# A decoder layer on one core: gates by tanh, differential-head products in token layout, work moved from VectorE to ScalarE

## The chip, the cores and the metric

The kernel runs on one core of one Trainium2 chip. The metric is the device time of one execution in microseconds (us). Before the change it is 731.5 us, the median of three runs (731.49 to 732.18).

A core has five instruction streams that run side by side and wait for one another through semaphores: TensorE (PE; its weight loads are shown apart as PEld), VectorE (DVE), ScalarE (ACT), GpSimd (POOL) and SyncE (SP, which here only issues weight transfers). Each stream is executed in its own order.

## The reference, cut to what matters

One layer, 512 tokens by 1024 features in float32. Two attention branches work on the same normalised input, are gated, merged, and followed by a gated MLP with a short convolution:

```python
h = rms_norm(x, g_mix)
z = h @ w_in                     # q, k, v of both branches and the gate logits gl
ya = swa_sink_attention(...)     # 8 heads, window 128, each query block sees 1 or 2 key blocks
ob = diff_attention(...)         # 4 heads, full causal: (softmax1 - lam * softmax2) @ v, v is 128 wide
yb = rms_norm(ob, subln_b) * (1 - lam_init)      # over the 128 features of a head, per token
gates = sigmoid(gl)
mixed = gates[0] * (ya @ w_br_a) + gates[1] * (yb @ w_br_b)
x = x + mixed @ w_o
h = rms_norm(x, g_ffn)
x = x + (silu(conv_g) * conv_v) @ w_down         # conv3 over h @ w_up
```

## The kernel before, in words

Every large product is done to float32 accuracy with three float32r matmuls: an operand is split into a high part (ACT, `whi`, line 123) and a low part (DVE or POOL, `wlo`, line 124), and `mm3` (lines 145 to 147) adds high*high, low*high and high*low. Weights come in units of 128x1024 through three raw buffers; a unit is split one unit ahead of its use.

Only TensorE's order is written out by hand. The other engines' instructions are ordered by the framework's scheduler, except where `issue_after` holds one behind another.

While attention runs, TensorE is kept supplied by a *filler*, the `Stream` object `fs`: a list of generators (gate projections, differential q/k/v projections, branch-A output, early branch-B output) that gives three 512-column matmuls per step. The table `FILL` says how many steps stand at each place between attention instructions. Its total is fixed by the work; the table only deals it out.

The stages, with the lines that the change touches:

- Sliding-window attention (8 units of a query block and a key/value head): `swa_score` (exponentials on ACT, line 581; the multiply by the reciprocal row sum, line 588, on DVE), `swa_trans` (transposes, line 597), `swa_av`.
- Gates: `gate(c)` projects one 128-feature chunk, and DVE multiplies it by the token norm into a buffer `g`. `sigmoids` (line 486) later applies the sigmoid in place: eight chunks as one block between the two attention stages, eight at the end of the second. `issue_after` keeps them behind the exponentials.
- Differential attention (16 units of head h and query block b): `diff_score` (line 683 exponentials, line 688 multiply by -lam over the sum, line 689 the difference), `diff_trans` (transposes, line 705, then the split into `ath`, line 712, and `atl`, line 713), and, once per head, `diff_av` (line 725: twelve matmuls of 512, 384, 256 and 256 columns, the values as weights, result with features on the partitions). A token's norm then needs a sum over partitions: `diff_rms` sums by matmuls with ones (line 173), and `diff_out` spreads the reciprocal root over the free axis with diagonal matrices (line 193) and two matmuls (line 194), then multiplies (line 740).
- `k_parts` builds key operands with a half copied across partitions by DVE (line 438).
- `mix` multiplies the second gate by the branch-B product (line 849), adds, splits; `resid` adds the input (line 876).

Of the kernel before, what the change touches and what calls it, by code (L numbers as in the profile page):

```python
# [62 lines left out]
FILL = dict(v=[9, 17, 25, 33], m=[0, 0, 0, 0], r=[4, 9, 13, 18], o=[7, 11, 15, 17], e=[1, 1, 0, 40], kv=4, up=3,  # L63
            warm=8, q=7, k=19, k2=4, s1=[0, 3, 2, 2, 2, 3, 3, 0, 0, 3], s2=[4, 3, 0, 3, 1, 7, 5, 2, 0, 1],
            s3=[3, 0, 1, 5, 6, 2, 2, 6, 0, 1], p0=4, p1=5, p2=8, ud=6, pd=[8, 9], f=[9, 0],
            a=[5, 1, 8, 7, 10, 2, 0, 3, 0, 1, 7, 4, 6, 0, 0, 5],
            b=[6, 2, 4, 4, 2, 7, 2, 1, 2, 0, 2, 0, 1, 1, 2, 2], c=[7, 0, 0, 1], d=[1, 0, 0, 5])
# [5 lines left out]
def tile_decoder_layer(ctx: ExitStack, tc: tile.TileContext, x4, wall, cst_d, relb_d, oneh_d, xn_d, out):  # L73
# [411 lines left out]
    def sigmoids(c0):  # L485
        return [nc.scalar.activation(G[c], G[c], AF.Sigmoid) for c in range(c0, c0 + 8)]
# [71 lines left out]
    swa_acts = []  # L558

    def swa_score(b, n):  # L560
# [22 lines left out]
        swa_acts.append(nc.scalar.activation(sk, sk, AF.Exp))  # L583
# [3 lines left out]
        for j in range(4):  # L587
            nc.vector.tensor_scalar(s[:, j, :W], s[:, j, :W], rc[:, j:j + 1], None, ALU.mult)
# [17 lines left out]
    def swa_av(b, n):  # L606

        if n == 0:
            swa_o[b] = otile()
        u = swa_o[b]  # L610
        ps = at()
        pT = swa_p.pop((b, n))
        for i, (t, h, _) in enumerate(pT):
            nc.tensor.matmul(ps, vhl[:, t, n, :], h, start=i == 0, stop=False)  # L614
        for i, (t, _, l) in enumerate(pT):
            nc.tensor.matmul(ps, vah[:, t, n, :], l, start=False, stop=i == len(pT) - 1)
        s, o = halves[n]
# [41 lines left out]
    exps = []  # L659

    def diff_score(h, b):
# [20 lines left out]
        for c in range(2):  # L682
            exps.append(nc.scalar.activation(p[:, c, :N], p[:, c, :N], AF.Exp, bias=nmx[:, c:c + 1],
                                             accum_out=sm[:, c:c + 1]))
# [3 lines left out]
        nc.vector.tensor_scalar(p[:, 1, :N], p[:, 1, :N], rc[:, 1:2], None, ALU.mult)  # L688
# [3 lines left out]
    def diff_trans(h, b):  # L692
        p = dp.pop((h, b))
        if b == 0:


            ath = at3.tile([P, 1664], F32R, tag="ath", name=nm("ath"), bufs=1)
            atl = at3.tile([P, 1664], F32R, tag="atl", name=nm("atl"), bufs=1)
            nc.gpsimd.memset(ath[:, 1408:1536].bitcast(F32), 0.0)
            nc.gpsimd.memset(atl[:, 1408:1536].bitcast(F32), 0.0)  # L700
            dt[h] = ath, atl
        ath, atl = dt[h]
# [3 lines left out]
        psv = ps[:, :(b + 1) * P].rearrange("p (a b) -> p a b", b=P)  # L706

        def cols(f):
            a = f[:, b * P:b * P + 1]
            return bass.AP(a.tensor, a.offset, [a.ap[0], (384, b + 1), (1, P)])  # L710

        nc.scalar.activation(cols(ath), psv, AF.Copy)
        nc.vector.tensor_tensor(cols(atl), psv, cols(ath.bitcast(F32)), ALU.subtract)
# [3 lines left out]
    def diff_av(h):  # L717
        ath, atl = dt.pop(h)
        po = at()

        for i, (part, at_) in enumerate(((0, ath), (1, ath), (0, atl))):
            for kb in range(NT):
                q0 = min(kb * P, 256)
                c0 = kb * 384 + q0
                nc.tensor.matmul(po[:, q0:S], vb[kb][part][:, h * P:(h + 1) * P], at_[:, c0:c0 + S - q0],  # L725
                                 start=i == 0 and kb == 0, stop=i == 2 and kb == NT - 1)
        sq = otile()
        nc.scalar.activation(sq, po, AF.Square)
        o = otile()
        nc.scalar.activation(o, po, AF.Copy, scale=gsub)  # L730
        dpo[h] = o, sq

    def diff_rms(h):
        o, sq = dpo[h]
        dpo[h] = o, token_rsqrt(token_sums(sq, lambda: fs.fill(1)), P)

    def diff_out(h):
        o, col = dpo.pop(h)
        r = along_free(col, otile, lambda: fs.fill(FILL["m"][h]))
        nc.vector.tensor_tensor(o, o, r, ALU.mult)  # L740
        nc.scalar.activation(ybt[0][:, h, :], o, AF.Copy)
        nc.vector.tensor_tensor(ybt[1][:, h, :], o, ybt[0][:, h, :].bitcast(F32), ALU.subtract)
# [26 lines left out]
    sig = ExitStack()  # L769
    with tc.issue_after(swa_acts[-1].ins), tc.issue_after(swa_acts[-2].ins):  # L770
        for i in sigmoids(0):
            sig.enter_context(tc.issue_after(i.ins))
# [5 lines left out]

    def products(place):
        for h in range(4):  # L780
            if FILL["v"][h] == place:
                fs.until("vb")
                diff_av(h)
                fill("c", h)

    todo = [(h, b) for h in range(4) for b in range(NT)]
    for i in range(len(todo) + 1):
# [25 lines left out]
    sig.close()  # L813
    fs.until("gb")
    with tc.issue_after(exps[-1].ins), tc.issue_after(exps[-2].ins), tc.issue_after(exps[-3].ins):
        sigmoids(8)
# [31 lines left out]
    def mix(c, ps):  # L848
        nc.vector.tensor_tensor(G[8 + c], ps, G[8 + c], ALU.mult)  # L849
# [22 lines left out]
    def resid(c, ps):  # L872
# [3 lines left out]
        nc.vector.tensor_tensor(t, ps, xr, ALU.add)  # L876
# [183 lines left out]
```

## Time and profile before

| | |
|---|---|
| median of three runs | 731.5 us |
| profiled execution, its own time | 730.34 us |
| its span, first to last instruction | 728.6 us |
| mean granted TensorE clock | 0.993 of full |
| PE busy | 705.9 us (97%) |
| DVE, ACT, POOL busy | 450.0, 316.0, 167.0 us |

Matmuls are pipelined: one 512-column matmul is shown with 0.39 us, but the next starts 0.23 us after it. What a matmul costs a full queue is therefore the distance between starts, and a duration is that plus the time its result takes to come out. A time in square brackets is how long the engine sat idle before the instruction, and which engine's instruction ended that.

### The profile page before, as it was taken

What the parts mean: (1) busy time and instruction counts of PE and PEld (TensorE: products, weight loads), DVE (VectorE), ACT (ScalarE), POOL (GpSimd) and SP (SyncE); (2) the same over time, 40 slices, a digit from 0 to 9 for tenths busy, and PEclk for the clock granted to TensorE, in tenths of its full rate; (3) what the DMA queues carried; (4) which work ended last, traced back from release to release, by engine and by line L of the source; (5) the groups of instructions that cost most, each with busy time, mean ns of one, the idle gap of its engine ahead of it and who ended that gap; (6) DMA issues with size and microseconds to landing.
All of it is one profiled execution on the core that took longest, in us unless ns stands there. A gap on an engine that the chain in (4) does not pass through costs nothing.

```text
span 728.6 us, 8960 instructions
## 1 busy us (share of the span) xinstructions
PE 705.9 (97%) x3312; PEld 582.6 (80%) x3312; DVE 450.0 (62%) x940; ACT 316.0 (43%) x522; POOL 167.0 (23%) x130
## 2 busy tenths in 40 slices
PE   8999999789999999989999999999999999999998
PEld 5888788668887778768888888888888888888888
DVE  5787797737429898685448877676676674322220
ACT  6554666854236446334426444444444442121220
POOL 1145253254446220274300210110110110000000
PEclk9999999989999999999999999999999999999999
DMA  8762202032221110235421332323323223333310
GB/s 315 289 207 88 87 30 88 0 116 87 72 99 62 58 59 30 87 107 167 132 87 58 116 117 91 111 86 96 107 87 102 101 80 101 125 107 108 109 66 30
DMA packets 21820, 74.04 MB, mean 102 GB/s; under 512 B 2612, under 2 KB 3152, under 8 KB 21648
## 3 DMA queue, kind: packets, MB, share of 16 engines
q1 hardware_dynamic: 18976, 65.02, 26.4%
q0 software_dynamic: 1360, 6.34, 2.6%
q10 hardware_dynamic: 1440, 2.11, 0.8%
q8 instruction: 26, 0.43, 0.2%
q14 instruction: 18, 0.15, 0.1%
HBM read 71.34 MB, written 4.47 MB: 104 GB/s over the span
## 4 chain that ended last, share of the span: by engine, by line
PE 78%; DVE 8%; issue 2%; ACT 2%; POOL 0%; DVEq 0%; ACTq 0%; POOLq 0%
PE pj L145 24%; PE pj L147 24%; PE pj L146 24%; PE at L725 1%; DVE g L850 1%; PE at L597 1%; PE at L444 1%; DVE g L849 1%; DVE o L193 1%; PE at L443 1%; DVE p L678 1%; DVE p L689 1%; PE at L705 1%; PE at L614 0%; DVE wlo L124 0%
## 5 line engine op out<-in xcount | busy, mean ns | idle before, releaser
L123 ACT ACTIVATE whi<-raw 128x1024 fp32r<-128x1024 f32 (+1 forms) x117 | 121.8, 1044 | 174.8 <-PE pj L146 115.9
L145 PE MATMUL pj<-xg,whi 128*128 128x512 f32 x480 | 189.6, 395 | 0.0
L147 PE MATMUL pj<-xg,wlo 128*128 128x512 f32 x480 | 187.3, 390 | 0.0
L146 PE MATMUL pj<-xg,whi 128*128 128x512 f32 x480 | 187.2, 390 | 0.0
L124 DVE TENSOR_TENSOR wlo<-raw,whi 128x1024 fp32r<-128x1024 f32 (+1 forms) x84 | 103.4, 1234 | 81.9 <-ACT whi L123 81.8
L147 PEld LDWEIGHTS pj<-xg,wlo 128*128 128x128 f32 x480 | 90.2, 188 | 19.2
L146 PEld LDWEIGHTS pj<-xg,whi 128*128 128x128 f32 x480 | 90.4, 188 | 17.7
L145 PEld LDWEIGHTS pj<-xg,whi 128*128 128x128 f32 x480 | 90.3, 188 | 17.5
L124 POOL TENSOR_TENSOR wlo<-raw,whi 128x1024 fp32r<-128x1024 f32 x33 | 79.6, 2418 | 96.2 <-ACT whi L123 86.7
L145 PE MATMUL pj<-whi,xg 128*128 128x512 f32 (+1 forms) x156 | 59.5, 382 | 6.0 <-ACT whi L123 5.9
L916 DVE TENSOR_TENSOR u<-pj,rbc 128x512 f32<-128x512 f32 x44 | 30.2, 689 | 48.3 <-PE pj L147 48.3
L146 PE MATMUL pj<-wlo,xg 128*128 128x512 f32 (+1 forms) x156 | 58.2, 373 | 1.7 <-POOL wlo L124 1.7
L147 PE MATMUL pj<-whi,xg 128*128 128x512 f32 (+1 forms) x156 | 58.1, 372 | 0.1
L145 PEld LDWEIGHTS pj<-whi,xg 128*128 128x128 f32 x156 | 29.8, 191 | 11.3 <-ACT whi L123 6.0
L919 ACT ACTIVATE yc<-u,cst 128x512 f32<-128x512 f32 x44 | 35.5, 810 | 4.5 <-DVE u L916 4.5
L145 PE MATMUL pj<-y,whi 128*128 128x512 f32 (+1 forms) x95 | 37.0, 390 | 0.0
L147 PE MATMUL pj<-y,wlo 128*128 128x512 f32 (+1 forms) x95 | 36.3, 382 | 0.2 <-POOL wlo L124 0.2
L147 PE MATMUL pj<-qv,wlo 128*128 128x512 f32 (+1 forms) x94 | 35.4, 377 | 1.1 <-DVE wlo L124 1.1
L146 PE MATMUL pj<-y,whi 128*128 128x512 f32 (+1 forms) x95 | 36.2, 381 | 0.0
L921 DVE SCALAR_TENSOR_TENSOR yc<-u,cst,yc 128x510 f32<-128x510 f32 x44 | 34.8, 794 | 1.3
L146 PEld LDWEIGHTS pj<-wlo,xg 128*128 128x128 f32 x156 | 29.9, 191 | 7.0 <-POOL wlo L124 2.2
L145 PE MATMUL pj<-qv,whi 128*128 128x512 f32 (+1 forms) x94 | 35.4, 376 | 0.0
(213 smaller groups left out, 1151.3 us busy)
## 6 DMA issues: line engine op xcount, KB each, us to landing
raw<-in_w_dram SPq DMA_DIRECT2D x109, 512.0 KB, 3.3
raw<-in_w_dram SPq DMA_DIRECT2D x8, 384.0 KB, 3.1
scr<-scr POOLq DMA_DIRECT2D x1, 2304.0 KB, 11.4
xnat<-in_xn_dram SPq DMA_DIRECT2D x2, 1024.0 KB, 9.4
tmp<-in_x_dram POOLq DMA_DIRECT2D x8, 256.0 KB, 3.2
g<-in_x_dram SPq DMA_DIRECT2D x7, 256.0 KB, 6.7
out_dram<-x ACTq DMA_DIRECT2D x7, 256.0 KB, 2.0
bias_a<-scr POOLq DMA_DIRECT2D x1, 1024.0 KB, 7.3
```

What stands on the lines that cost most here:

```text
L123: nc.scalar.activation(hi[:, :width], raw[:, :width], AF.Copy)
L124: eng.tensor_tensor(lo[:, :width], raw[:, :width], hi[:, :width].bitcast(F32), ALU.subtract)
L145: nc.tensor.matmul(ps, a[0], b[0], start=start, stop=False)
L146: nc.tensor.matmul(ps, a[0], b[1], start=False, stop=False)
L147: nc.tensor.matmul(ps, a[1], b[0], start=False, stop=stop)
L193: nc.vector.tensor_scalar(dg[:, t * P:(t + 1) * P], ident, part[:, t:t + 1], None, ALU.mult)
L443: nc.tensor.matmul(ps, q[:, qsl], kh[:, ksl], start=True, stop=False)
L444: nc.tensor.matmul(ps, q[:, qsl], kl[:, ksl], start=False, stop=True)
L597: nc.tensor.transpose(ps[:, j * P:(j + 1) * P], s[:, j, kb * P:(kb + 1) * P], ident)
L916: nc.vector.tensor_tensor(u, ps, rbc2, ALU.mult)
L919: nc.scalar.activation(y, u, AF.Identity, bias=cst[:, C_CB + ch:C_CB + ch + 1], scale=cw[2])
L921: nc.vector.scalar_tensor_tensor(y[:, 2:S], u[:, 0:S - 2], cw[0], y[:, 2:S], ALU.mult, ALU.add)
```

## The change

- The sigmoid is computed as (1 + tanh(x/2))/2. The tanh is issued with each gate chunk; the "+1" is joined to the multiply that uses the gate (`scalar_tensor_tensor`), and the half is applied once in `resid`. The two blocks of sigmoids and the `issue_after` around them go.
- A differential head's product is done per unit (h, b): the transposed probabilities are the weights, the values move, 128 columns each, and the result has tokens on the partitions. The sum of squares comes from ACT's accumulator; the reciprocal root scales per partition (two blocks on ACT, two on DVE); four transposes bring a head back to features on partitions, and the split out of PSUM applies the per-feature gain.
- Half of the sliding-window multiplies, the multiply by -lam over the sum, and the copies across partitions in `k_parts` move from DVE to ACT.
- `ath` and `atl` are three buffers of 512 columns instead of one of 1664 each; eight short POOL memsets go.
- `FILL` is dealt out anew. The number of filler matmuls is the same.

```diff
+        for k, (s, o) in zip(kh, halves):
+            nc.scalar.activation(k[o, :], ps[s, :], AF.Copy, scale=g[s])
         for k, l, (s, o) in zip(kh, kl, halves):
-            nc.vector.tensor_copy(k[o, :], k[s, :].bitcast(F32))
...
         nc.vector.tensor_tensor(t, ps, rbc, ALU.mult)
+        nc.scalar.activation(t, t, AF.Tanh, scale=0.5)
...
-            nc.vector.tensor_tensor(G[c], ps, G[c], ALU.mult)
+            nc.vector.scalar_tensor_tensor(G[c], G[c], 1.0, ps, ALU.add, ALU.mult)
...
         for j in range(4):
-            nc.vector.tensor_scalar(s[:, j, :W], s[:, j, :W], rc[:, j:j + 1], None, ALU.mult)
+            if j % 2:
+                nc.scalar.activation(s[:, j, :W], s[:, j, :W], AF.Copy, scale=rc[:, j:j + 1])
+            else:
+                nc.vector.tensor_scalar(s[:, j, :W], s[:, j, :W], rc[:, j:j + 1], None, ALU.mult)
...
-        nc.vector.tensor_scalar(p[:, 1, :N], p[:, 1, :N], rc[:, 1:2], None, ALU.mult)
+        nc.scalar.activation(p[:, 1, :N], p[:, 1, :N], AF.Copy, scale=rc[:, 1:2])
...
+    def diff_av(h, b):
+        ath, atl = dt.pop((h, b))
+        if b == 0:
+            dpo[h] = otile(), stat.tile([P, NT], F32, tag="oss", name=nm("oss"))
+        o, ss = dpo[h]
+        po = at()[:, :P]
         for i, (part, at_) in enumerate(((0, ath), (1, ath), (0, atl))):
-            for kb in range(NT):
-                q0 = min(kb * P, 256)
-                c0 = kb * 384 + q0
-                nc.tensor.matmul(po[:, q0:S], vb[kb][part][:, h * P:(h + 1) * P], at_[:, c0:c0 + S - q0],
+            for kb in range(b + 1):
+                nc.tensor.matmul(po, at_[:, kb * P:(kb + 1) * P], vb[kb][part][:, h * P:(h + 1) * P],
...
+        ob = o[:, b * P:(b + 1) * P]
+        nc.scalar.activation(ob, po, AF.Square, accum_out=ss[:, b:b + 1])
+        nc.scalar.activation(ob, po, AF.Copy)
 
     def diff_rms(h):
-        o, sq = dpo[h]
-        dpo[h] = o, token_rsqrt(token_sums(sq, lambda: fs.fill(1)), P)
+        o, ss = dpo[h]
+        r = token_rsqrt(ss, P)
+        for b in range(NT):
+            ob = o[:, b * P:(b + 1) * P]
+            if b % 2:
+                nc.vector.tensor_scalar(ob, ob, r[:, b:b + 1], None, ALU.mult)
+            else:
+                nc.scalar.activation(ob, ob, AF.Copy, scale=r[:, b:b + 1])
 
     def diff_out(h):
-        r = along_free(col, otile, lambda: fs.fill(FILL["m"][h]))
-        nc.vector.tensor_tensor(o, o, r, ALU.mult)
+        for b in range(NT):
+            nc.tensor.transpose(ps[:, b * P:(b + 1) * P], o[:, b * P:(b + 1) * P], ident)
+        nc.scalar.activation(ybt[0][:, h, :], ps, AF.Copy, scale=gsub)
...
-        nc.vector.tensor_tensor(t, ps, xr, ALU.add)
+        nc.vector.scalar_tensor_tensor(t, ps, 0.5, xr, ALU.mult, ALU.add)
```

Of the table, the entry for the steps after each product (`c`) went from four numbers to sixteen, and a new entry says from which unit on products start:

```diff
-            b=[6, 2, 4, 4, 2, 7, 2, 1, 2, 0, 2, 0, 1, 1, 2, 2], c=[7, 0, 0, 1], d=[1, 0, 0, 5])
+            b=[6, 2, 4, 4, 2, 7, 2, 1, 2, 2, 0, 0, 1, 4, 2, 2], c=[3, 0, 0, 0, 2, 0, 0, 0, 2, 1, 0, 0, 1, 0, 0, 0],
+            d=[1, 0, 0, 5], v0=4)
```

How instructions moved, at three places. Line numbers of the changed kernel differ by a few; in a row stand the line, the operation, the destination, its sources and the shape of the destination, on matmuls the shape streamed.

First, ScalarE between the two attention stages, before the change: the last key parts of the second differential head, the sigmoids of the first eight gates (`g`), the high part of a weight unit (`whi_1611`), the exponentials of the first differential unit (`p`).

```order
L436 ACTIVATE qv_1588<-at_1580,cst 64x512
L486 ACT_TABLE_LOAD
L486 ACTIVATE g_666<-g_666 128x512
...
L486 ACTIVATE g_1526<-g_1526 128x512
L123 ACTIVATE whi_1611<-raw_1609 128x1024
L683 ACT_TABLE_LOAD
L683 ACTIVATE p_1639,dsm_1641<-p_1639,dnmx_1650 128x128 x2
```

After the change, the same place:

```order
L476 ACTIVATE g_1507<-g_1507 128x512
...
L437 ACTIVATE qv_1595<-at_1588,cst 64x512
L437 ACTIVATE qv_1596<-at_1588,cst 64x512
L439 ACTIVATE qv_1595<-at_1588,cst 64x512
L439 ACTIVATE qv_1596<-at_1588,cst 64x512
L124 ACTIVATE whi_1711<-raw_1709 128x1024
L685 ACTIVATE p_1651,dsm_1653<-p_1651,dnmx_1662 128x128 x2
L690 ACTIVATE p_1651<-p_1651,drc_1666 128x128
```

The two table loads and the eight sigmoids are gone from between the key parts and the weight unit; two copies of key parts (L439) and the multiply by -lam over the sum (L690) are new. The eighth tanh (L476) stands earlier, among the last sliding-window instructions.

Second, TensorE at the last differential head's product, before the change (once per head; `at_3008` is the result, `ath` and `atl` the moving parts, `vbh` and `vbl` the weights):

```order
L725 MATMUL at_3008<-ath_2831,vbh_1830 128x512
L725 MATMUL at_3008<-ath_2831,vbh_1834 128x384
L725 MATMUL at_3008<-ath_2831,vbh_1838 128x256
L725 MATMUL at_3008<-ath_2831,vbh_1842 128x256
L725 MATMUL at_3008<-ath_2831,vbl_1831 128x512
...
L725 MATMUL at_3008<-atl_2832,vbh_1842 128x256
```

After the change, one unit's product is an own group (this is head 2, block 3; a head has groups of 3, 6, 9 and 12), close behind the transposes (L701) of the same unit and the scores (L445, L446) of the next:

```order
L701 MATMUL at_2891<-ident,p_2766 128x128 x4
L445 MATMUL at_2901<-qv_2582,qv_2569 128x256
L446 MATMUL at_2901<-qv_2580,qv_2569 128x256
L445 MATMUL at_2905<-qv_2583,qv_2570 128x256
L446 MATMUL at_2905<-qv_2581,qv_2570 128x256
L718 MATMUL at_2918<-vbh_1830,ath_2889 128x128
L718 MATMUL at_2918<-vbh_1834,ath_2889 128x128
...
L718 MATMUL at_2918<-vbh_1842,atl_2890 128x128
```

The values have become the moving operand, every matmul has 128 columns, and no filler stands between these transposes and the product that needs them.

Third, ScalarE at that same unit, before the change: the split `ath` of the transposes follows a weight unit, and the evacuation of the product (L728, L730) stands behind it.

```order
L683 ACTIVATE p_2740,dsm_2742<-p_2740,dnmx_2751 128x128 x2
L123 ACTIVATE whi_2907<-raw_2905 128x1024
L712 ACTIVATE ath_2555<-at_2787 128x4x128
L728 ACTIVATE o_2807<-at_2794 128x512
L730 ACTIVATE o_2809<-at_2794,gsub 128x512
```

After the change, the evacuation of the previous unit's product (L721 the squares, L722 the copy) stands ahead of the split (L702):

```order
L721 ACTIVATE o_2729,oss_2730<-at_2877 128x128
L722 ACTIVATE o_2729<-at_2877 128x128
L702 ACTIVATE ath_2889<-at_2891 128x512
L685 ACTIVATE p_2898,dsm_2900<-p_2898,dnmx_2909 128x256 x2
L690 ACTIVATE p_2898<-p_2898,drc_2913 128x256
L721 ACTIVATE o_2729,oss_2730<-at_2918 128x128
L702 ACTIVATE ath_2933<-at_2935 128x128
```

ScalarE now does two evacuations per unit instead of two per head, and the split that TensorE waits for is queued behind them.

## Rows read from the trace of the kernel before

**Rows 1.** The page: each engine's busy time, its share of the span, and its instructions.

```profile
PE 705.9 (97%) x3312; PEld 582.6 (80%) x3312; DVE 450.0 (62%) x940; ACT 316.0 (43%) x522; POOL 167.0 (23%) x130
```

**Rows 2.** The view of waits, TensorE only: whom it waited for, us in total, times, longest.

```profile
PE pj L145 <- ACT whi L123: 5.9, 1, 5.9
PE pj L146 <- POOL wlo L124: 1.7, 1, 1.7
PE at L597 <- DVE s L588: 1.5, 1, 1.5
PE pj L146 <- POOL qv L853: 1.4, 2, 0.7
PE at L705 <- DVE p L689: 1.3, 2, 1.0
...
PE at L444 <- DVE qv L439: 1.0, 2, 0.5
PE at L194 <- DVE o L193: 0.7, 1, 0.7
PE at L725 <- ACT ath L712: 0.7, 1, 0.7
PE at L443 <- DVE qv L438: 0.6, 2, 0.4
```

**Rows 3.** The timeline from 140 to 153 us, PE, ACT and POOL: start, duration, engine, line.

```profile
140.18 1.28 ACT L486 ACT_TABLE_LOAD   x1
...
140.57 0.27 PE L444 MATMUL at<-qv,qv 128*128 128x128 f32 x1
...
141.48 4.26 ACT L486 ACTIVATE g<-g 128x512 f32<-128x512 f32 x8
...
145.65 1.04 ACT L123 ACTIVATE whi<-raw 128x1024 fp32r<-128x1024 f32 x1
...
146.74 0.79 PE L145 MATMUL pj<-whi,xg 128*128 128x512 f32 x1 [5.89 <-ACT whi L123]
...
149.22 0.79 PE L146 MATMUL pj<-wlo,xg 128*128 128x512 f32 x1 [1.69 <-POOL wlo L124]
...
152.25 0.40 PE L147 MATMUL pj<-whi,xg 128*128 128x512 f32 x1
```

**Rows 4.** Timelines of TensorE alone, for the distances between starts: 128-column float32r matmuls (from 70.39; five starts from 70.39 to 70.95) and the filler behind them, eight transposes (103.83 to 104.62), one head's product (186.29 to 188.25), plain filler (188.25 to 188.48), and a token sum between filler matmuls (192.81 to 193.50: two filler matmuls and one sum).

```profile
70.39 0.28 PE L444 MATMUL at<-qv,qv 128*128 128x128 f32 x1
...
70.95 0.27 PE L443 MATMUL at<-qv,qv 128*128 128x128 f32 x1
...
71.17 0.45 PE L145 MATMUL pj<-whi,xg 128*128 128x512 f32 x1
71.46 0.40 PE L146 MATMUL pj<-wlo,xg 128*128 128x512 f32 x1
...
103.83 1.03 PE L597 MATMUL at<-ident,s 128*128 128x128 f32 x8
104.62 0.48 PE L145 MATMUL pj<-xg,whi 128*128 128x512 f32 x1
...
186.29 0.80 PE L725 MATMUL at<-ath,vbh 128*128 128x512 f32 x4
...
188.25 0.40 PE L145 MATMUL pj<-y,whi 128*128 128x512 f32 x1
188.48 0.39 PE L146 MATMUL pj<-y,whi 128*128 128x512 f32 x1
...
192.81 0.40 PE L147 MATMUL pj<-y,wlo 128*128 128x512 f32 x1
...
193.50 0.39 PE L146 MATMUL pj<-y,whi 128*128 128x512 f32 x1
```

**Rows 5.** Groups of instructions with shapes kept apart: count, busy us, mean ns of one, idle time before.

```profile
L588 DVE TENSOR_SCALAR s<-s,rc 128x256 f32<-128x256 f32 x24 | 6.8, 350 | 0.1
...
L588 DVE TENSOR_SCALAR s<-s,rc 128x128 f32<-128x128 f32 x8 | 6.1, 828 | 0.1
...
L683 ACT ACTIVATION_READ_ACCUMULATOR p<-p,dnmx 128x1 f32 x32 | 6.0, 187 | 0.0
...
L881 DVE SCALAR_TENSOR_TENSOR xg<-x,cst,xg 128x512 fp32r<-128x512 f32 x8 | 6.0, 746 | 0.0
...
L849 DVE TENSOR_TENSOR g<-pj,g 128x512 f32<-128x512 f32 x8 | 5.1, 679 | 2.4 <-PE pj L863 2.4
...
L683 ACT ACTIVATE p<-p,dnmx 128x128 f32<-128x128 f32 x8 | 3.1, 394 | 2.7 <-DVE dnmx L681 2.6
...
L712 ACT ACTIVATE ath<-at 128x512 fp32r<-128x512 f32 x4 | 2.4, 598 | 8.0 <-PE at L705 7.9
...
L712 ACT ACTIVATE ath<-at 128x256 fp32r<-128x256 f32 x4 | 1.6, 400 | 1.9 <-PE at L705 1.8
...
L712 ACT ACTIVATE ath<-at 128x128 fp32r<-128x128 f32 x4 | 1.1, 270 | 4.6 <-issue 4.6
```

**Rows 6.** One stretch of 15 us: busy time of PE, PEld, DVE, ACT and POOL (with instruction counts), granted clock, DMA share, GB/s.

```profile
240.00:255.00 15.00, 14.37 (x73) 12.55 (x74) 11.57 (x41) 8.11 (x18) 3.75 (x5) 0.89 0.16 63
```

**Rows 7.** The timeline of DVE at the last head's norm: its first instruction (the mean square), and the one behind its last.

```profile
296.15 0.16 DVE L180 TENSOR_SCALAR tv<-at 128x4 f32<-128x4 f32 x1 [3.00 <-PE at L173]
...
298.52 0.17 DVE L187 CAST colh<-y 128x4 fp32r<-128x4 f32 x1
```

More of the change, by code (lines that the diff above doesn't have):

```diff
@@ L482, in br_a @@
                 yield
-            nc.vector.tensor_tensor(G[c], ps, G[c], ALU.mult)
-    def sigmoids(c0):
-        return [nc.scalar.activation(G[c], G[c], AF.Sigmoid) for c in range(c0, c0 + 8)]
+            nc.vector.scalar_tensor_tensor(G[c], G[c], 1.0, ps, ALU.add, ALU.mult)
     class Stream:
@@ L693, in diff_trans @@
         p = dp.pop((h, b))
[L694 to L702, printed above, removed]
+        N = (b + 1) * P
+        ath = at3.tile([P, S], F32R, tag="ath", name=nm("ath"), bufs=3)
+        atl = at3.tile([P, S], F32R, tag="atl", name=nm("atl"), bufs=3)
         ps = at()
@@ L733, in diff_rms @@
-    def diff_rms(h):
-        o, sq = dpo[h]
-        dpo[h] = o, token_rsqrt(token_sums(sq, lambda: fs.fill(1)), P)
-    def diff_out(h):
-        o, col = dpo.pop(h)
-        r = along_free(col, otile, lambda: fs.fill(FILL["m"][h]))
-        nc.vector.tensor_tensor(o, o, r, ALU.mult)
-        nc.scalar.activation(ybt[0][:, h, :], o, AF.Copy)
-        nc.vector.tensor_tensor(ybt[1][:, h, :], o, ybt[0][:, h, :].bitcast(F32), ALU.subtract)
+        nc.scalar.activation(ath[:, :N], ps[:, :N], AF.Copy)
@@ new lines, in diff_trans @@
+        nc.vector.tensor_tensor(atl[:, :N], ps[:, :N], ath[:, :N].bitcast(F32), ALU.subtract)
+        dt[h, b] = ath, atl
+    dpo = {}
+    def diff_av(h, b):
[4 more added lines that the diff above has]
+        po = at()[:, :P]
+        for i, (part, at_) in enumerate(((0, ath), (1, ath), (0, atl))):
+            for kb in range(b + 1):
+                nc.tensor.matmul(po, at_[:, kb * P:(kb + 1) * P], vb[kb][part][:, h * P:(h + 1) * P],
+                                 start=i == 0 and kb == 0, stop=i == 2 and kb == b)
+        ob = o[:, b * P:(b + 1) * P]
+        nc.scalar.activation(ob, po, AF.Square, accum_out=ss[:, b:b + 1])
+        nc.scalar.activation(ob, po, AF.Copy)
@@ new lines, in diff_rms @@
+    def diff_rms(h):
+        o, ss = dpo[h]
[6 more added lines that the diff above has]
+                nc.scalar.activation(ob, ob, AF.Copy, scale=r[:, b:b + 1])
+    def diff_out(h):
+        o, _ = dpo.pop(h)
+        ps = at()
+        for b in range(NT):
+            nc.tensor.transpose(ps[:, b * P:(b + 1) * P], o[:, b * P:(b + 1) * P], ident)
+        nc.scalar.activation(ybt[0][:, h, :], ps, AF.Copy, scale=gsub)
+        nc.vector.scalar_tensor_tensor(ybt[1][:, h, :], ps, gsub, ybt[0][:, h, :].bitcast(F32), ALU.mult,
+                                       ALU.subtract)
@@ L768, in tile_decoder_layer @@
     fs.until("ga")
[L769 to L772, printed above, removed]
     fs.parts += [("vb", project(U_VB, 512, vbb), lambda: vb_parts(vbb))]
@@ L777, in tile_decoder_layer @@
     fill("p2")
[L779 to L784, printed above, removed]
     todo = [(h, b) for h in range(4) for b in range(NT)]
@@ L798, in tile_decoder_layer @@
         if i > 0:
-            products(2 * i)
+            for u, hb in enumerate(todo):
+                if u < len(todo) - 1 and max(u + 2, FILL["v0"]) == i:
+                    fs.until("vb")
+                    diff_av(*hb)
+                    fill("c", u)
             diff_trans(*todo[i - 1])
             fill("b", i - 1)
-            products(2 * i + 1)
+            if i == len(todo):
+                diff_av(*todo[-1])
         for step, at_unit in ((diff_rms, FILL["r"]), (diff_out, FILL["o"])):
@@ L812, in tile_decoder_layer @@
                         fs.parts += [("bb", br_b_early(), None)]
-    sig.close()
     fs.until("gb")
-    with tc.issue_after(exps[-1].ins), tc.issue_after(exps[-2].ins), tc.issue_after(exps[-3].ins):
-        sigmoids(8)
     fs.until("bb")
@@ L848, in mix @@
     def mix(c, ps):
-        nc.vector.tensor_tensor(G[8 + c], ps, G[8 + c], ALU.mult)
+        nc.vector.scalar_tensor_tensor(G[8 + c], G[8 + c], 1.0, ps, ALU.add, ALU.mult)
         nc.vector.tensor_tensor(G[c], G[c], G[8 + c], ALU.add)
```

33 lines of the change are left out of this document (8 added, 25 removed).

## Prediction

> **What bounds the kernel now.** I read the page first: TensorE is busy 97% of the span, every other engine under 63% [rows 1]. So time is gained only where TensorE has nothing to do, works at the lower clock, or has less to do. The view of waits for TensorE alone comes second: it puts names on the idle time. The largest by far is one wait of 5.9 us for the high part of a weight unit on ScalarE, with 1.7 us behind it for the low part on GpSimd; the rest are many waits of 0.2 to 1.5 us for DVE in the two attention stages, and some in the merge [rows 2]. The timeline around the large one comes third. The reader is to see there that TensorE's last matmul starts at 140.57, that ScalarE loads a table and computes eight sigmoids meanwhile, and that the weight unit's high part starts only at 145.65 [rows 3]. Last come the distances between starts, the price of a matmul on a full queue: 0.23 us for 512 columns, 0.112 for 128 columns ((70.95 - 70.39)/5), 0.10 for a 128-column transpose (0.79/8) [rows 4].
>
> **The change part by part.** The sum is made against the profiled execution, 730.3 us, which is 1.2 below the median of 731.5; the 1.2 is added again at the end.
>
> *The block of sigmoids: -9.7.* From 140.57 to 152.25 TensorE issues the matmul at 140.57 and eight filler matmuls, worth 0.11 + 8 x 0.23 = 2.0 us; 11.7 have passed [rows 3]. So 9.7 are lost: the wait for the high part, the wait for the low part that POOL can only begin after it, and a restart below full clock. In the changed order there is neither table load nor sigmoid between the key parts and the weight unit. The eight tanh stand one by one behind their gate chunks, each like a sigmoid (4.26 us for eight, start to end [rows 3]), in a stage where TensorE has filler. What is late next: the key parts of two differential heads, now eight copies on ScalarE instead of four there and four on DVE, and behind them on ScalarE's queue the weight unit `whi_1711` and the first exponentials. The table deals ten filler steps (ten times 0.69 us) and sixteen transposes (1.6 us) over them, so I price this at zero, and at +5 if that cover fails. A tanh can also hold ScalarE's queue while it waits for DVE's multiply; then the next weight unit is late. It is ordered one unit ahead, so zero, up to 1 us each time otherwise. SyncE's weight loads keep their order; a load that waited for a buffer held through the stall starts earlier. POOL loses eight short memsets that nobody waited for: zero.
>
> *Sliding-window attention: -1.5.* TensorE waits 1.5 us for the multiply of line 588 [rows 2], which takes four DVE instructions per unit. Two go to ScalarE and run beside the other two. A 256-column multiply took 0.350 us on DVE, a 128-column one 0.828; a ScalarE copy of those widths out of PSUM took 0.400 and 0.270 [rows 5]. I take the whole wait as gone; the bounds are 0 and -1.5.
>
> [...]
>
> *Differential attention, waits: -2.9.* The old waits there are 1.3 for the difference `p`, 1.0 and 0.6 for key parts, 0.7 for line 193 and 0.7 for `ath`: 4.3 [rows 2]. [...] In that stage DVE sheds the multiply of line 688, the key copies, the eight diagonal multiplies per head and line 740; so I let all 5.9 go.
>
> New waits come in their place. A unit's product needs `ath` from ScalarE, and the unit before it puts a square with accumulator and a copy out of PSUM ahead of it. Where no filler stands between (head 2, block 3), TensorE has four transposes and four 256-column scores to do, 0.40 + 0.48 = 0.9 us by the starts; ScalarE has 0.394 + 0.187 + 0.270, then the split, 0.598 [rows 5]: 1.45, and some 0.16 until a result is out (0.39 shown against 0.23 between starts [rows 4]). So TensorE waits 0.7. The next unit, with one filler step there, I put at 0.7 too. Queued behind a waiting product are the next unit's transposes and scores, and on ScalarE its exponentials. Other units have two to nine steps of filler there: zero. A head's four transposes wait for the norm, twelve small DVE instructions that took 298.52 - 296.15 = 2.4 us [rows 7], and for two scalings on ScalarE at 0.27 each [rows 5]. At the last head that makes, with square and accumulator, 3.5 us and three hand-overs of 0.16, so 4.0, against fifteen filler matmuls, 3.45: 0.5, and all of the merge stands behind it. At head 2 the scalings queue behind two 384-column exponentials: 1.1. Sum of the new ones 3.0; bounds 0 and 22 (see the rivals).
>
> *TensorE's own work: +2.9.* Products: 120 matmuls of 128 columns x 0.112 = 13.4, against 4 x (188.25 - 186.29) = 7.8: +5.6. Token sums: two filler matmuls with one sum between took 0.69, so a sum is worth 0.23; 16 go: -3.7. The eight matmuls of line 194 at 0.23: -1.8. Sixteen transposes at 0.10: +1.6. Behind a 128-column group the first filler matmul takes 0.29 instead of 0.23; twenty such groups: +1.2 [rows 4]. For the products the bounds are half a 128-column distance, 0.06 (if loading the weights hid fully), which is -6.2, and the 0.112 that every such row shows; a load that did not overlap at all would be +9, but no row has that.
>
> [...]
>
> *Merge: +0.5.* Eight multiplies become `scalar_tensor_tensor`: 0.746 against 0.679 us [rows 5], in a stretch where TensorE waits for the chain of DVE and POOL (1.4 us for the split of line 853 alone [rows 2]): 8 x 0.067. In the residual eight more lie beside 24 matmuls each: zero. The wait itself stays.
>
> Sum: -9.7 - 1.5 - 2.9 + 2.9 + 0.5 = -10.7. 730.3 - 10.7 = 719.6, plus 1.2: 720.8 us.
>
> **The rivals.**
>
> *Slower: ScalarE's queue sets the pace.* Each of 16 units now crosses from DVE to ScalarE and back once more, for the multiply by -lam over the sum, and has two evacuations on ScalarE. If every unit made TensorE wait 0.7 us for `ath` and 0.7 for `p`, the new waits would be 22.4 instead of 3.0: 720.8 + 19.4 = 740.2. It turns the result slower from 0.86 us per unit on (3.0 + 10.7 = 13.7, over 16). For it: ScalarE's queue is in order, and a weight unit of 1.04 us [rows 3] can stand ahead of any of these steps. Against it: ScalarE was busy 8.1 of 15 us at 240 to 255 [rows 6], and most units have filler to cover. [...]
>
> *Half: the stall only moves.* The block of sigmoids goes, but what stood behind it, key parts and the low part on POOL (2 to 3 us after the high part: 149.22 against 146.74 [rows 3]), is late itself by half of 9.7, and DVE's old waits are replaced in full by ScalarE's: 720.8 + 4.85 + 2.9 = 728.6. For it: the weight unit's place in the order is still behind all key parts.
>
> *More: no new waits, and products closer.* New table and buffers hide all of it: 720.8 - 3.0 = 717.8, and at 0.09 us per product matmul, between the bounds, 715.
>
> *No change: the block was covered.* If whatever follows had been late anyway, the 9.7 buy nothing and the rest cancels: 731. Against it: TensorE's other waits in that view are 7.2 us together, spread over both attention stages and the merge [rows 2], so little else was due just then.
>
> **How the numbers follow.** Forecast 0.60, half 0.15, more 0.12, slower 0.09, no change 0.04. The likeliest one gives 720.8; its own range is 717 to 725. The range for 8 in 10 takes in "more" at its lower end and "half" at its upper: 714 to 729. About 0.2% (1.5 us) is what a measurement of this kernel can tell from no change: faster by over that 0.86, within it 0.05, slower 0.09.
>
> **What would show it.** In the changed kernel's waits, line 123's successor should be gone as a wait of several us, and no stretch between 135 and 165 us should show TensorE under 14 us busy of 15. Line 718's 128-column matmuls should start 0.11 us apart. TensorE should wait for lines 702 and 730 to 732, together some 3 us, and no longer for the key parts. DVE's busy total should fall and ScalarE's rise. Wrong would be the forecast if TensorE waited for lines 690, 691 or 702 in most units, or if the stage from the first differential scores to the merge took longer than before.

## The result, and the profile after

The changed kernel takes 721.9 us (median of 4 runs, 721.64 to 723.62), the kernel before beside it 731.8 (4 runs): a ratio of 0.9867, 95% interval 0.9848 to 0.9886. The forecast was 720.8. The profiled execution took 721.64 us with a span of 719.7, against 730.34 and 728.6 before: 8.7 us less, where the prediction's sum, made on that execution, had 10.7.

The page, as in [rows 1]: VectorE lost 24.5 us of busy time, ScalarE gained 23.8, and TensorE's share rose to 98%.

```profile
PE 704.2 (98%) x3360; PEld 583.8 (81%) x3360; DVE 425.5 (59%) x862; ACT 339.8 (47%) x609; POOL 164.8 (23%) x122
```

The view of waits, TensorE only, which answers to [rows 2]:

```profile
PE at L718 <- ACT ath L702: 2.2, 1, 2.2
PE at L701 <- DVE p L691: 1.6, 2, 1.3
PE pj L147 <- POOL qv L843: 1.4, 2, 0.7
...
PE at L617 <- ACT pth L603: 0.8, 2, 0.5
PE at L446 <- DVE qv L441: 0.8, 1, 0.8
...
PE at L600 <- DVE s L591: 0.4, 1, 0.4
```

The 5.9 us for the weight unit and the 1.7 for its low part are gone. The wait for the multiply of the sliding-window stage fell from 1.5 to 0.4 us. The merge's 1.4 us stands unchanged. New at the top is one wait of 2.2 us for `ath`, in one unit of sixteen. The wait for line 193 is gone. The view has none for lines 730 to 732 either, which the prediction had named.

Windows of 15 us, with the columns of [rows 6]. The stretch of the old stall (135 to 165) runs at full clock. So does 240 to 255, which was at 0.89. The lower clock now stands from 270 to 285, behind the wait for `ath`. From 135 to 150 TensorE is busy 13.68 us, a little under the 14 that the prediction had named as a sign.

```profile
135.00:150.00 15.00, 13.68 (x71) 11.31 (x69) 9.52 (x18) 11.68 (x20) 5.53 (x6) 1.00 0.16 56
150.00:165.00 15.00, 15.00 (x69) 12.45 (x70) 11.13 (x34) 8.81 (x19) 6.64 (x3) 1.00 0.23 79
...
240.00:255.00 15.00, 15.00 (x82) 12.87 (x81) 10.74 (x43) 12.21 (x30) 3.43 (x3) 1.00 0.16 55
...
270.00:285.00 15.00, 14.98 (x73) 12.27 (x72) 10.53 (x47) 10.15 (x32) 0.00 (x0) 0.89 0.14 44
```

To put all of it on one scale, I took from each distance between two starts on TensorE what the shape takes on a full queue (0.227 us for 512 columns, 0.119 for 256, 0.111 for 128, 0.1085 for a 128-column transpose, 0.64 for four matmuls of an old product). What is left over is time lost to waits, to the clock and to changes of shape. What was taken off adds up to TensorE's own work. This is worked out from the timelines and good to about 1 us (the same work comes out at 690.0 to 691.5), and kernels of other length shift a little against the bounds of a stretch.

| kernel | lost 60–135 us | 135–160 | 160–335 | own work | median ratio to before |
|---|---|---|---|---|---|
| before | 3.6 | 9.8 | 15.1 | 690.6 | 1 |
| changed | 4.4 | 1.8 | 10.7 | 693.1 | 0.9867 |
| tanh alone | 3.7 | 6.0 | 16.6 | 690.1 | 0.9954 |
| filler numbers alone | 3.2 | 11.9 | 15.2 | 690.8 | 1.0009 |
| tanh and these numbers | 4.1 | 1.5 | 14.7 | 691.5 | 0.9909 |
| changed, sigmoids back | 3.2 | 14.1 | 12.3 | 693.7 | 1.0055 |
| changed, multiplies back on VectorE | 4.3 | 1.0 | 10.3 | 693.1 | 0.9856 |
| changed, old table | 4.4 | 5.9 | 14.9 | 693.2 | 0.9989 |
| changed, old layout | 4.1 | 1.8 | 28.9 | 690.8 | 1.0083 |
| the same, old places | 4.4 | 1.8 | 25.9 | 690.0 | 1.0030 |
| the same, and multiplies back | 4.1 | 1.0 | 26.9 | 690.4 | 1.0049 |

From before to changed: own work +2.5, the stretch of the stall -8.0, what lies behind it -4.4, the sliding-window stage +0.8; with the rest, +0.2, this is the span's -8.9.

### The profile page after: what moved, and what is told of

Same layout as the page of the kernel before. It is cut to its first block, busy times and chain, and to the rows that moved or that the text cites. A ratio compares the mean times of both kernels' runs of the same rounds, so it can differ in the third digit from the quotient of the medians.

```text
span 719.7 us, 9050 instructions
## 1 busy us (share of the span) xinstructions
PE 704.2 (98%) x3360; PEld 583.8 (81%) x3360; DVE 425.5 (59%) x862; ACT 339.8 (47%) x609; POOL 164.8 (23%) x122
## 4 chain that ended last, share of the span: by engine, by line
PE 87%; ACT 5%; DVE 5%; issue 1%; DMA 1%; SPq 0%; ACTq 0%; DVEq 0%
PE pj L146 27%; PE pj L148 27%; PE pj L147 27%; PE at L718 1%; DVE g L840 1%; ACT p L685 1%; PE at L446 1%; DMA g<-in_x_dram 1%; PE at L445 1%; PE at L416 1%; PE at L600 1%; DVE g L839 1%; DVE wlo L125 1%; ACT qv L439 1%; ACT qv L437 1%
## 5 line engine op out<-in xcount | busy, mean ns | idle before, releaser
L146 PE MATMUL pj<-whi,xg 128*128 128x512 f32 (+1 forms) x156 | 58.4, 374 | 1.1 <-ACT xg L260 1.1
L148 PE MATMUL pj<-whi,xg 128*128 128x512 f32 (+1 forms) x156 | 57.6, 369 | 0.1
L916 ACT ACTIVATE yc<-yc 128x512 f32<-128x512 f32 x22 | 13.9, 632 | 44.1 <-DVE yc L911 44.1
```

The lines of the kernel that those rows point to most:

```text
L146: nc.tensor.matmul(ps, a[0], b[0], start=start, stop=False)
L148: nc.tensor.matmul(ps, a[1], b[0], start=False, stop=stop)
L916: nc.scalar.activation(yg, yg, AF.Silu)
```

## Experiments

**1. Tanh alone** (on the kernel before).

```diff
+        nc.scalar.activation(t, t, AF.Tanh, scale=0.5)
-            nc.vector.tensor_tensor(G[c], ps, G[c], ALU.mult)
+            nc.vector.scalar_tensor_tensor(G[c], G[c], 1.0, ps, ALU.add, ALU.mult)
-        for i in sigmoids(0):
...
-        sigmoids(8)
```

> The kernel before with one part of the change: gates by tanh behind each chunk, (1 + tanh) in the two multiplies, 0.5 in the residual; the output layout, the multiplies and copies and the filler table stay as before. My theory: the block of sigmoids was worth its 9.7 us by itself and costs 0.5 in the merge, so 731.8 - 9.2 = 722.6 (ratio 0.987), with no wait over 2 us left between 135 and 155 us of the trace. Rival, the stall only moves: without the new filler table and the key copies on ScalarE, the key parts behind the block are late by half of it, so 727 (0.994), and the wait shows at the key parts or at the weight unit. Rival, the gain came from the other parts: above 730.

Measured: 728.37 us, ratio 0.9954 (0.9940 to 0.9968). My theory falls: 3.9 us, not 9.2. The block is gone, but 6.0 of its 9.8 us are lost again behind it: 1.5 in a wait for the key parts of line 439, 1.7 for the first `p`, and the lower clock that follows (0.89 from 150 to 165 us). The timeline shows why the key parts are late:

```profile
143.10 2.39 POOL L124 TENSOR_TENSOR wlo<-raw,whi 128x1024 fp32r<-128x1024 f32 x1 [2.04 <-issue]
...
143.69 2.08 DVE L438 CAST qv<-qv 64x512 fp32r<-64x512 f32 x1
...
145.79 0.74 DVE L439 SCALAR_TENSOR_TENSOR qv<-at,cst,qv 64x512 fp32r<-64x512 f32 x1
...
147.88 0.35 PE L443 MATMUL at<-qv,qv 128*128 128x256 f32 x1 [1.50 <-DVE qv L439]
```

The same copy takes 0.42 us at 146.54. Here it starts inside GpSimd's subtraction of a weight unit and ends 0.28 us after that does.

**2. The sigmoids put back** (into the changed kernel).

> The changed kernel with the two blocks of sigmoids put back, all else as changed. My theory: the stall comes back whole, 721.9 + 9.7 - 0.5 = 731 (ratio 0.999), since nothing else in the change touches it. Rival: ScalarE, now with eight key copies and half of the multiplies beside the block, stalls for longer, 734 or more. Rival, the new filler table hides part of the block: 726.

Measured: 735.71 us, ratio 1.0055 (1.0039 to 1.0071): the first rival, ScalarE stalls for longer. Against the changed kernel the block costs 13.8 us. ScalarE's timeline, and the matmul that waits:

```profile
137.54 1.38 ACT L439 ACTIVATE qv<-at,cst 64x512 fp32r<-64x512 f32 x2
...
141.75 1.38 ACT L439 ACTIVATE qv<-at,cst 64x512 fp32r<-64x512 f32 x2
143.15 1.28 ACT L488 ACT_TABLE_LOAD   x1
144.44 4.26 ACT L488 ACTIVATE g<-g 128x512 f32<-128x512 f32 x8
148.61 2.93 ACT L124 ACTIVATE whi<-raw 128x1024 fp32r<-128x1024 f32 x3
...
149.70 0.79 PE L146 MATMUL pj<-whi,xg 128*128 128x512 f32 x1 [9.05 <-ACT whi L124]
```

Two pairs of key copies, 1.38 us a pair (line 439, a pair for each of two heads), now stand ahead of the block: 2.8 us of the 3.2 by which the wait grew from 5.89.

**3. Multiplies and copies back on VectorE** (in the changed kernel): lines 589, 690 and 439 as before the change.

> The changed kernel with the moved multiplies and copies back on VectorE: all four multiplies of a sliding-window unit, the multiply by -lam over the sum, the second key copies. My theory: the waits that the prediction let go come back, 1.5 us for the multiply in the sliding-window stage and 1.5 to 2.9 for the difference p and the key parts: 724 to 726 (ratio 0.990 to 0.993). [...] Rival: all of it was hidden, 721.9.

Measured: 721.24 us, ratio 0.9856 (0.9841 to 0.9870). That overlaps the changed kernel's interval: the move to ScalarE is worth nothing that can be measured here. My theory (724 to 726) falls: the waits that I had put down to VectorE did not come back. The one for the sliding-window multiply stays at 0.4 us, as in the changed kernel. What the version loses at one place it gains at another: at 148 us TensorE waits 0.5 for `p` instead of 1.3, at 64.8 it no longer waits for key parts, but between 70 and 80 it loses 1.4 more.

**4. The old output layout** (in the changed kernel), first with the new places of the norms, then with the old places, then also with the multiplies back on VectorE.

```diff
-        po = at()[:, :P]
+        po = at()
...
-                nc.tensor.matmul(po, at_[:, kb * P:(kb + 1) * P], vb[kb][part][:, h * P:(h + 1) * P],
+                nc.tensor.matmul(po[:, q0:S], vb[kb][part][:, h * P:(h + 1) * P], at_[:, c0:c0 + S - q0],
```

> The changed kernel with the differential heads' output in the old layout (one product per head with 512 columns, the norm by token sums and a row along the free axis), tanh, moved multiplies and the filler table kept, the filler of the products dealt to four places. By the prediction's terms TensorE's own work is 2.9 us less and the new waits for ath (2.2 us, and about 1.6 of lower clock behind it) go, while the old waits for DVE in that stage come back only in part (up to 2.5): 717.5 to 720 (ratio 0.981 to 0.984). Rival: the layout pays for itself by what it takes off DVE (eight 512-column multiplies by the diagonal per pair of heads and a 512-column multiply), so without it 724 or more.

> The changed kernel with the old output layout, as in the run that gave 737.6, but the norms, their rows along the free axis and the filler around these at the places of the kernel before (two to three units between a norm and its row instead of one). If the 15.7 us of that run came from the places (7.9 us of waits for the diagonal multiplies of line 194), it falls to 722 to 726 (ratio 0.987 to 0.992). If the layout itself is worth much, because it takes the diagonal multiplies off VectorE and the wait for the product of a whole head off the path, it stays above 728 (0.994). By the prediction's terms alone (own work 2.5 less, waits for ath gone): below 721 (0.985).

> The kernel of the run that gave 733.6 (changed kernel, output in the old layout, norms at the old places) with the moved multiplies and key copies back on VectorE. Against the changed kernel with the multiplies on VectorE (721.2) it differs by layout and table alone. If the multiplies on ScalarE are what the old layout cannot stand (ScalarE's queue ahead of the split of a whole head's rows), it falls to the level of tanh with part of the table, 724 to 726 (ratio 0.990 to 0.993), and the layout's worth is 3 to 5 us. If the old layout itself costs it, it stays at 731 or more (0.999).

Measured: 737.64 us (1.0083, 1.0068 to 1.0098), 733.63 (1.0030, 1.0018 to 1.0042) and 735.47 (1.0049, 1.0033 to 1.0064). All three lie far above what I had expected; of the rivals, those hold that put the loss on the old layout. Waits of the first, of the second and of the third:

```profile
PE at L195 <- DVE o L194: 7.9, 6, 4.0
```

```profile
PE at L707 <- DVE p L691: 4.9, 4, 1.9
PE at L707 <- DVE coll L189: 3.4, 1, 3.4
PE at L727 <- ACT ath L714: 3.3, 2, 2.9
```

```profile
PE at L195 <- DVE o L194: 3.8, 3, 1.8
PE at L444 <- DVE qv L439: 3.3, 2, 3.2
PE at L704 <- DVE colh L188: 2.5, 1, 2.5
```

With one unit between a norm and its row, TensorE waits 7.9 us for the diagonal multiplies. With the old places the norm's small instructions and the whole head's `ath` are late instead. Neither engine for the multiplies mends it. The old layout's own work is 2.3 to 3.1 us less, as the prediction had it, but in this table it loses 15 to 18 us more.

**5. The old filler table** (in the changed kernel; only the places of the norms, `r`, and the products' filler, `c`, stay new; the places of the heads' outputs, `o`, are the old ones as well).

> The changed kernel with the filler table of the kernel before, except the norms' places and the products' filler, which the new layout needs. After tanh alone gave only 3.9 us of the 9.7, my theory is that the table gives the rest: with the old one the waits for key parts and for the first difference p come back between 140 and 155 us, and waits for ath where the new table had put steps: 724.5 to 727 (ratio 0.990 to 0.993). Rival: the key copies on ScalarE and the new layout do it, whatever the table: 722 (0.9867).

Measured: 730.43 us, ratio 0.9989 (0.9978 to 1.0000), over 3 us above the upper end of my range. All else in the change is there, and 8.5 of its 9.9 us (730.4 against 721.9) are gone: 4.1 between 135 and 160 us, 4.2 after it.

```profile
PE at L696 <- DVE p L686: 3.3, 1, 3.3
PE at L441 <- DVE qv L436: 2.4, 3, 1.3
PE at L713 <- ACT ath L697: 2.3, 3, 1.1
```

**6. Part of the new table, with tanh and without** (on the kernel before). Two steps move from behind head 0's key parts to behind head 1's, and the sliding-window stage gets others (its entries add up to 74 steps instead of 70):

```diff
-            s1=[0, 3, 2, 2, 2, 3, 3, 0, 0, 3], s2=[4, 3, 0, 3, 1, 7, 5, 2, 0, 1], s3=[3, 0, 1, 5, 6, 2, 2, 6, 0, 1]
+            s1=[0, 3, 0, 3, 2, 4, 4, 0, 0, 3], s2=[2, 3, 0, 5, 1, 7, 5, 5, 0, 0], s3=[3, 0, 2, 5, 6, 2, 2, 6, 0, 1]
-            p0=4, p1=5, p2=8
+            p0=4, p1=3, p2=10
```

> The kernel before with tanh and with the new filler numbers up to the first scores of the differential heads (s1, s2, s3, p1, p2); layout, multiplies and the rest of the table as before. My theory: two more steps behind the key parts of head 1 cover the rest of the stall (1.5 us for the key parts, 1.7 for the first p): 728.4 - 2 to 3 = 725.5 to 726.5 (ratio 0.991 to 0.992). Rival: the key copies on VectorE, 2.08 us for one beside GpSimd's subtraction in the run with tanh alone, take longer than two steps cover, and 728 stays (0.995).

> The kernel before with the new filler numbers up to the first scores (s1, s2, s3, p1, p2) and nothing else: the sigmoid blocks stay. Tanh alone gave 3.9 us and tanh with these numbers 6.5. If the 2.6 between them is a cover that only counts once the block is gone, the numbers alone give nothing: 730.5 to 733 (ratio 0.999 to 1.002), with the wait of 5.9 us for the weight unit still there. If they are a gain of their own (waits in the sliding-window stage that go), 728 to 729.5 (0.995 to 0.997).

Measured: 725.05 us with tanh (0.9909, 0.9895 to 0.9922), just under my range, and 732.0 without (1.0009, 1.0000 to 1.0018). Without tanh the old wait still stands, but the one for the sliding-window multiply (line 584 here), 1.5 us before, has shrunk to 0.4:

```profile
PE pj L141 <- ACT whi L119: 6.3, 1, 6.3
...
PE at L593 <- DVE s L584: 0.4, 2, 0.2
```

Tanh alone gives 3.9 us, the numbers alone nothing in all, both 6.5: the cover counts only once the block is gone. With both, the key copy is just as slow (1.92 us), but TensorE has two more steps to do, and 1.5 us are lost between 135 and 160 instead of 6.0.

**7. Each product computed twice** (in the changed kernel).

> The changed kernel with every product of the differential heads computed twice in a row into the same tile, the second run overwriting the first: 120 more matmuls of 128 columns, so the time holds work that the result does not need. Price of one, by the prediction (start to start on a full queue, 0.112 us): 721.9 + 13.4 = 735.3 (ratio 1.005). [...] Rival, the columns alone (0.06): 729 (0.996). Up to 1 us less each if the added matmuls cover part of a wait.

Measured: 736.86 us, ratio 1.0071 (1.0059 to 1.0083): 14.9 us more between the profiled executions (736.51 - 721.64), 0.124 for each of 120 added matmuls. In the products' groups the starts lie 0.110 us apart at full clock (23.4 us over 213 distances), which makes 13.2 for 120. Twelve more distances, behind the same wait for `ath`, are 0.21 us: there the clock fell further, and most of the rest stands there:

```profile
270.00:285.00 15.00, 12.92 (x74) 12.11 (x73) 9.30 (x39) 7.71 (x26) 0.00 (x0) 0.79 0.18 61
```

**8. Cover for the wait for `ath`** (in the changed kernel: three steps moved), and the same idea with the multiplies on VectorE (two steps there, one each at two other places).

```diff
-            a=[6, 1, 7, 8, 10, 2, 0, 5, 0, 2, 7, 3, 6, 0, 0, 5],
-            b=[6, 2, 4, 4, 2, 7, 2, 1, 2, 2, 0, 0, 1, 4, 2, 2]
+            a=[6, 1, 7, 8, 10, 2, 0, 5, 0, 2, 7, 3, 6, 3, 0, 5],
+            b=[6, 2, 4, 4, 2, 7, 2, 1, 2, 2, 0, 0, 1, 1, 2, 2]
```

> The changed kernel with three filler steps (0.69 us each) moved at one place: from behind the transposes of head 3, block 1 to ahead of the product of head 2, block 3, where TensorE waits 2.2 us for ath. My theory: the whole wait goes, and the lower clock from 270 to 285 us behind it (0.89, worth about 1.6 by the same reckoning as in the prediction): 721.9 - 2.2 to 3.8 = 718.1 to 719.7 (ratio 0.981 to 0.984). Rival: the wait only moves to the next product (head 3, block 0) or to the difference p, which lose the steps: 721.5 or more (0.986).

> The changed kernel with the moved multiplies and copies back on VectorE (721.2) and six filler numbers changed: two steps ahead of the product of head 2, block 3, one step each ahead of the first transposes and of head 2's first scores. It is the version that should be the fastest: 721.2 - 1.1 (ath) - 0.5 (first p) - 0.5 (key parts) - up to 1 (clock) = 718 to 719.5 (ratio 0.981 to 0.983). If the waits only move, 721 or more (0.985).

Measured: 721.15 us (0.9857, 0.9841 to 0.9874) and 722.92 (0.9874, 0.9858 to 0.9890). My theory falls in both. The 1.6 us for the lower clock in the first is an estimate, 11% of 15 us at a granted 0.89. The waits move, as the rivals had it, though the first time lies between theory and rival (719.7 and 721.5). The waits of the first:

```profile
PE at L738 <- ACT o L732: 1.2, 1, 1.2
PE at L718 <- ACT ath L702: 1.2, 2, 0.7
```

The 2.2 us at head 2, block 3 went and the clock stayed at 1.00 up to 285 us, but the next product, head 2's transposes and a later product wait instead. In the second, the loss between 135 and 160 us fell to 0.2, and at 253 a wait of 1.4 us behind a norm's small instructions came up. None of the versions is measurably faster than the changed kernel.

## Why the prediction was right, and where it was not

The median was right within 1.1 us, the sum on the profiled execution within 2.0, and both partly by luck: errors of up to 2.6 us in the terms cancel.

*The block of sigmoids, -9.7: in the changed kernel -8.0, but not from tanh by itself.* The mechanism was right, with its condition: without the two filler steps what is late next costs 4.5 us more (6.0 lost against 1.5), close to the "+5 if that cover fails". The changed kernel has the cover, but "so I price this at zero" is 1.8 us too low there. Of these, 1.3 are a wait for the first `p`, which had no term. The timeline of GpSimd, VectorE and TensorE:

```profile
145.24 2.40 POOL L125 TENSOR_TENSOR wlo<-raw,whi 128x1024 fp32r<-128x1024 f32 x1 [5.65 <-issue]
...
146.14 1.52 DVE L683 TENSOR_SCALAR dnmx<-dmx 128x2 f32<-128x2 f32 x1
...
149.90 0.33 PE L701 MATMUL at<-ident,p 128*128 128x128 f32 x1 [1.32 <-DVE p L691]
```

A negation of two columns, 0.17 us elsewhere, took 1.52: it ended at 147.66, when GpSimd's subtraction ended (147.64). In experiment 3 the same negation met no subtraction, took 0.17, and the wait was 0.5 us.

*Sliding-window attention, -1.5: +0.8.* The wait for the multiply went nearly as forecast (1.5 to 0.4 us), but not for the reason given, "Two go to ScalarE": it is 0.4 as well with all multiplies on VectorE (experiment 3), and with nothing changed but filler numbers (experiment 6). With the multiplies moved and the old table it is 0.8 (experiment 5). So the new numbers suffice, and that this term's wait came out is luck. Two losses came: 0.8 for key parts at 64.8, behind ScalarE's two further copies, which I had priced at zero, and 1.6 between 128 and 135 us. Of the latter some 0.7 comes with the new numbers alone; the rest is two waits for `pth`, 0.8 together. They stand in the runs with tanh and these numbers, with the multiplies on either engine, and neither with the numbers alone nor with the sigmoids put back. ScalarE's queue and the second wait in the changed kernel:

```profile
129.96 1.06 ACT L124 ACTIVATE whi<-raw 128x1024 fp32r<-128x1024 f32 x1
...
131.92 0.62 ACT L476 ACTIVATE g<-g 128x512 f32<-128x512 f32 x1
132.44 0.59 ACT L603 ACTIVATE pth<-at 128x512 fp32r<-128x512 f32 x1
...
133.08 0.50 PE L617 MATMUL at<-pth,vhl 128*128 128x512 f32 x1 [0.50 <-ACT pth L603]
```

A weight unit and a tanh stand ahead of the split `pth`. With the sigmoids put back neither stands there, and the same split starts at 131.57 instead of 132.44. The prediction had named a tanh in ScalarE's queue as a danger, but only for the next weight unit, and had priced it at zero.

The price of the moved multiplies was also too low. I took 0.27 to 0.40 us from copies out of PSUM without a scale. The multiplies read SBUF and take a scale for each partition:

```profile
L589 ACT ACTIVATE s<-s,rc 128x256 f32<-128x256 f32 x12 | 5.4, 500 | 3.0 <-DVE rc L586 3.0
...
L722 ACT ACTIVATE o<-at 128x128 f32<-128x128 f32 x16 | 4.4, 276 | 0.3
...
L690 ACT ACTIVATE p<-p,drc 128x512 f32<-128x512 f32 x4 | 2.9, 720 | 1.1 <-DVE drc L689 1.1
L732 ACT ACTIVATE o<-o,y 128x128 f32<-128x128 f32 x8 | 2.8, 392 | 6.0 <-DVE y L164 6.0
L739 ACT ACTIVATE y<-at,gsub 128x512 fp32r<-128x512 f32 x4 | 2.7, 679 | 0.5 <-PE at L738 0.5
...
L626 ACT ACTIVATE y<-o 128x512 fp32r<-128x512 f32 x4 | 2.5, 629 | 1.6 <-DVE o L622 1.6
...
L702 ACT ACTIVATE ath<-at 128x512 fp32r<-128x512 f32 x4 | 2.4, 594 | 0.2 <-PE at L701 0.2
...
L730 DVE TENSOR_SCALAR o<-o,y 128x128 f32<-128x128 f32 x8 | 1.9, 284 | 0.2
...
L690 ACT ACTIVATE p<-p,drc 128x128 f32<-128x128 f32 x4 | 1.6, 398 | 1.5 <-DVE drc L689 1.5
```

By these rows ScalarE took longer than VectorE for a multiply of the same shape: 500 ns against 350 at 256 columns [rows 5], 398 against 284 at 128 (line 730). The prediction's 828 ns for 128 columns on VectorE was a mean of three multiplies of 0.28 us and one of 2.46 (last section). What the move costs in instructions does not show in the kernel's time, as experiment 3 shows.

*Differential attention, waits: -2.9, and 1.2 for boundaries, which the prediction booked under own work and the table counts as lost, together -1.7; measured -4.3 up to 300 us, good to about 1.* Of the 5.9 us of old losses that the prediction let go, 1.6 stood for the lower clock. No run shows that term as a time of its own; shown are a granted 0.89 from 240 to 255 us [rows 6], of which 11% of 15 us would make 1.6, an estimate, and 1.00 there after the change. The size was too small and the reason wrong: "DVE sheds the multiply of line 688, the key copies" is not why the old waits go, since they stay away with all of it back on VectorE. By experiments 4 and 5 neither the layout alone makes them go (old table: 4.2 more lost than in the changed kernel) nor the table alone. The layout without its table brings its 2.5 us of own work and no gain. With it there is one: tanh, numbers and old layout (725.05) against tanh, the whole table and the new layout, multiplies on VectorE in both (721.24), differ by 3.8. Whether the old layout with a table dealt out for it could do as well was not tried.

*The wait for `ath`: 0.7 forecast, 2.2 measured, and the clock behind it.* The place was right (head 2, block 3), the size not. ScalarE's queue there:

```profile
265.37 1.04 ACT L124 ACTIVATE whi<-raw 128x1024 fp32r<-128x1024 f32 x1
266.31 0.39 ACT L690 ACTIVATE p<-p,drc 128x128 f32<-128x128 f32 x1
266.61 0.61 ACT L476 ACTIVATE g<-g 128x512 f32<-128x512 f32 x1
267.13 0.25 ACT L721 ACTIVATE o<-at 128x128 f32<-128x128 f32 x1
...
267.50 0.28 ACT L722 ACTIVATE o<-at 128x128 f32<-128x128 f32 x1
267.68 0.59 ACT L702 ACTIVATE ath<-at 128x512 fp32r<-128x512 f32 x1
```

I counted the square and the copy; a weight unit, a multiply by -lam over the sum and a tanh stood ahead of them, 1.8 us from start to start. The lower clock behind it (0.89 over 15 us, some 1.6 us as 11% of it, an estimate) had no term. The three other new waits of the sum (0.7, 0.5 and 1.1) did not come.

*Own work: +2.9 with the boundaries, 1.7 without; measured +2.5.* The products' price holds: 0.110 us from start to start over 213 distances. The bound of +9 had no source beside it; the weight loads (lines 145 to 147) are shown with 188 ns in the view of before, and (188 - 112) ns for each of 120 makes 9.1 us, an estimate.

*Merge: +0.5; measured -0.1.* The new form took 676 ns, the old one 679 [rows 5]:

```profile
L839 DVE SCALAR_TENSOR_TENSOR g<-g,pj 128x512 f32<-128x512 f32 x8 | 5.1, 676 | 2.1 <-PE pj L853 2.1
```

The rivals: ScalarE's queue did not set the pace, since TensorE waited for `ath` once and for `p` twice, 3.8 us together. "The stall only moves" is what tanh alone does. That its time (728.4) lies so near the rival's (728.6) is chance, since the rival's sum holds the rest of the change as well. That the block was covered, or that all new waits were hidden, fits none of the runs. Against the first the prediction counted 7.2 us of other waits; the whole view of before has 11.4, which changes nothing in the argument.

## What to carry to other kernels

Where filler is dealt out by hand, price a removed stall together with the table: here the same edits gave 9.9 us with the new numbers and 1.1 with the old ones, and part of the numbers alone gave nothing. When a wait goes as forecast, undo the edit that was to remove it; here the wait for the sliding-window multiply stayed away. When a queue sets a wait, list everything in it from the releasing event on, weight loads and deferred gates too, not only the instructions of the step itself. An edit that shifts work between two engines off the path (18 us of VectorE's busy time in experiment 3) may be worth nothing, so put it back and measure.

## Hardware behaviour that was not expected

VectorE copies and small `tensor_scalar` out of SBUF that ran into GpSimd's work on SBUF tiles took longer, and most ended only behind it. The 64x512 copy takes 0.42 us alone. Beside GpSimd's subtraction it took 1.12 and 1.66 us (before), 2.08 (tanh alone) and 2.51, each time the overlap plus 0.28. The longest, from the run with the multiplies back on VectorE:

```profile
233.55 2.40 POOL L125 TENSOR_TENSOR wlo<-raw,whi 128x1024 fp32r<-128x1024 f32 x1 [4.23 <-ACT whi L124]
...
233.72 2.51 DVE L439 CAST qv<-qv 64x512 fp32r<-64x512 f32 x1
```

In the third run of experiment 4 a copy that began 0.34 us ahead of a subtraction took its 0.42. A copy beside a `memset` on GpSimd took longer too, 0.52: in the run of the fence a copy that began at 139.50, beside memsets until 139.73, ended at 140.02. The 828 ns of the 128-column multiplies [rows 5] came about in the same way: before, both groups of four ran into a subtraction and took 3.05 us each, three multiplies of 0.28 and a fourth of 2.46 that ended 0.08 us after it; with them back on VectorE one group had none beside it and took 0.87 us.

ScalarE's activations took longer with a scale for each partition, and longer out of SBUF than out of PSUM. At 512 columns one took 0.59 us out of PSUM without such a scale and 0.68 with one, 0.63 out of SBUF without and 0.72 with (lines 702, 739, 626 and 690 above): some 0.09 for the scale and 0.04 for the place. At 128 columns the two together are the 0.12 between 0.27 to 0.28 and 0.39. The prices that the prediction took from copies had neither.
